# Outer taps of an MLP's depthwise convolution: over two sequences at once, with the two tokens at their border computed apart

## The chip, the cores and the metric

The kernel runs on one core of a Trainium2 chip. Its engines are TensorE (PE; PEld is its weight load), VectorE (DVE), ScalarE (ACT), GpSimd (POOL) and SyncE (SP), which issues all DMAs here. Each engine works through its own queue in order and waits on semaphores for the others. The metric is the device time of one execution in microseconds; the time of a kernel is the median of its runs.

## What is computed

Two layers of an encoder trunk run over two sequences with shared weights, one of 512 tokens and one of 256. Each layer has a mixer (state-space scan, retention, neighbourhood attention, gates) and then a gated MLP; only the MLP matters here. The convolution has three taps along the tokens of one sequence, each feature by itself, and zeros beyond both ends, so that nothing crosses from one sequence to the other.

```python
def dwconv(x, w, bias):                       # width 3, centred, per channel, zero padding
    ...
h2 = rmsnorm(x, norm_ffn)
u = dwconv(h2 @ ffn_w_up, ffn_conv_w, ffn_conv_b)       # 1024 -> 2 x 2816
val, gt = jnp.split(u, 2, axis=-1)
x = x + (jax.nn.silu(gt) * val) @ ffn_w_down            # 2816 -> 1024
```

## The kernel before

Both sequences lie side by side as T = 768 columns: columns 0 to 511 are the first (TP = 512), 512 to 767 the second. In the MLP the features stand on the 128 partitions and the tokens on the free axis. The 2816 features of each half are 22 tiles of 128, and `up(i)` makes one tile of the value half (`rv`) and one of the gate half (`rg`) together; one such call is called a unit below.

- **Products.** `pair_products` (L500) computes both tiles by a Strassen-like scheme: seven products of 12 matmuls each (`prod`, L489 to L494), 384 columns wide, which accumulate in PSUM tiles `acc` named X, Y, V, Z. The weights are split in two float32r parts, `whi` by ACT (L206) and `wlo` by DVE (L207), after DVE has formed sums of weight blocks in place (L217, L229). ACT and DVE take the results out of PSUM and combine them (all recorded at L498): into `pt`, `rv` and `rg`.
- **Convolution.** `conv(1)` treats `rg`, later `conv(0)` treats `rv`. ACT writes the middle tap and the bias for all 768 columns (L1285). DVE adds the left tap (L1287) and then the right one (L1289), each for the two sequences apart: 511 and 255 columns, since the first token of a sequence has no left neighbour and the last no right one. That makes four DVE operations for each tile. The gate half goes through Silu on ACT (L1293). Behind the value half DVE multiplies both (L1296), ACT rounds the product to `ah` (L1297) and DVE makes the remainder `al` (L1298).
- **Down projection.** Units are taken in groups of three (the last group of a layer has four): when a group's `ah` and `al` are there, PE multiplies them with the down weights into PSUM tiles `dn` (L1342 to L1344, 512 columns wide) and DVE adds these to `x` (L1357). The first unit of the next group is computed ahead of a group's down projection. In the last group of a layer eight `dn` tiles are begun with the first three units, and the last unit is added when it is there.

The order on each engine is not the order of the source: when the program is built, a scheduler with its own time model picks, from what the program's order and its priorities allow, the instruction to place next. So another set of instructions gives another interleaving. There are 2 x 22 = 44 units, hence 88 convolutions and 352 operations at L1287 and L1289.

Of the kernel before, what the change touches and what calls it, by code (L numbers as in the profile page):

```python
# [9 lines left out]
AF = mybir.ActivationFunctionType  # L10
OP = mybir.AluOpType

P = 128
# [3 lines left out]
TP = 512  # L17
TS = 256
T = TP + TS
# [264 lines left out]
def body(tc, nc, a, depth=DEPTH):  # L284
# [8 lines left out]
    act, tt, stt, ts = (nc.scalar.activation, nc.vector.tensor_tensor,  # L293
                        nc.vector.scalar_tensor_tensor, nc.vector.tensor_scalar)
# [79 lines left out]
    RANGES = ((0, TP), (TP, TS))  # L374
# [34 lines left out]
    def st4(name):  # L409
        return base.tile([P, 1024], F32, name=name, tag="st4", bufs=2)  # L410

    def small(shape, name, bufs=4):
        return base.tile(shape, F32, name=name, tag="sm_" + name, bufs=bufs)
# [174 lines left out]
    def layer(l, x_in, prev_x):  # L588
# [633 lines left out]
        for b in range(3):  # L1222
            dst, k0 = oT[b]
            r = [h[:, k0:k0 + 4, :] for h in dst]
# [28 lines left out]
        def ftile(name, tag, bufs=1, dt=F32):  # L1253
            return (ap if tag in ("ah", "al") else fp).tile([P, T], dt, name=name, tag=tag, bufs=bufs)
# [20 lines left out]
        def up(i):  # L1275

            raw = [ftile("rv", "rv"), ftile("rg", "rg")]
            us = {}
            out = [ftile("ah", "ah", 4, F32R), ftile("al", "al", 4, F32R)]

            def conv(s):
                r, u = raw[s], ftile("u", ("uv", "ug")[s])
                f = i + NFF * s
                w = lambda j: par[:, O_FW + f * 3 + j:O_FW + f * 3 + j + 1]
                act(u, r, AF.Identity, scale=w(1), bias=par[:, O_FB + f:O_FB + f + 1])  # L1285
                for c0, n in RANGES:
                    stt(u[:, c0 + 1:c0 + n], r[:, c0:c0 + n - 1], w(0), u[:, c0 + 1:c0 + n],  # L1287
                        op0=OP.mult, op1=OP.add)
                    stt(u[:, c0:c0 + n - 1], r[:, c0 + 1:c0 + n], w(2), u[:, c0:c0 + n - 1],  # L1289
                        op0=OP.mult, op1=OP.add)  # L1290
                us[s] = u
                if s == 1:
                    act(u, u, AF.Silu)  # L1293
                    return
                ah, al = out
                tt(u, u, us[1], op=OP.mult)  # L1296
                act(ah, u, AF.Copy)  # L1297
                tt(al, u, ah.bitcast(F32), op=OP.subtract)  # L1298

            pair_products(*raw, st4("pt"), conv, "po", first=todo[0]() if i == 0 else None)  # L1300
            return out
# [23 lines left out]
        for gi, g in enumerate(DOWN_GROUPS):  # L1325
# [9 lines left out]
            ws, n, end = W.get(len(g)), len(g), gi == len(DOWN_GROUPS) - 1  # L1335
# [64 lines left out]
```

## Time and profile before

| | |
|---|---|
| three runs | 2604.86, 2606.41, 2600.97 us; median 2604.86 us |
| the profiled execution | 2605.65 us, of which the traced span is 2603.9 us |
| PE busy in the span | 2560.1 us (98%) |
| DVE busy | 1904.2 us (73%) |
| ACT busy | 1153.4 us (44%) |
| POOL busy | 87.8 us (3%) |
| granted TensorE clock, mean | 0.995 of full speed |

The span is the traced part of one execution; the profiled execution's own time is 1.75 us longer than it. Busy times of one engine overlap with those of the others, so their shares don't add up. Matmuls are recorded longer than the distance at which they follow each other, since they are pipelined: whether PE has a pause is read from the starts.

### The profile page before, as it was taken

The page shows a single profiled execution, that of the slowest core. Times are in us where ns is not written, and L with a number is a line of the kernel's source. Part 1 is how long each engine was busy: PE and PEld are TensorE (multiplying, and loading weights), DVE is VectorE, ACT ScalarE, POOL GpSimd, SP SyncE. Part 2 cuts the span into 40 slices and gives each one's busy share as a digit, 9 for nine tenths or more (in the row PEclk, how much of TensorE's full clock was granted, in tenths as well). Part 3 has the DMA queues.
Part 4 walks back from the last instruction along what each step waited for, and adds up shares of the span by engine and source line. Part 5 has one row for each costly group of instructions (what it writes and reads, how often), then busy time and mean ns, then how long its engine had stood idle before and what let it go on. Part 6 is the DMA issues. An engine that isn't in the chain of part 4 may idle for free.

```text
span 2603.9 us, 37538 instructions
## 1 busy us (share of the span) xinstructions
PE 2560.1 (98%) x14290; PEld 2353.6 (90%) x14290; DVE 1904.2 (73%) x3204; ACT 1153.4 (44%) x1946; POOL 87.8 (3%) x130
## 2 busy tenths in 40 slices
PE   8999999999999999999999999999999999999998
PEld 8878999999889999999998789999998899999997
DVE  6758876665658887888866688765657598888887
ACT  5434465553235433333454455655432354333343
POOL 0002100000000000000000011100000000000000
PEclk9999999999999999999999999999999999999999
DMA  7356568747522222222453575787474222212222
GB/s 248 108 169 204 190 213 255 223 134 230 158 81 67 67 70 73 65 68 71 135 174 129 163 233 172 219 236 215 132 230 141 73 89 65 62 60 73 74 66 89
DMA packets 168900, 359.65 MB, mean 138 GB/s; under 512 B 16080, under 2 KB 62480, under 8 KB 168720
## 3 DMA queue, kind: packets, MB, share of 16 engines
q1 hardware_dynamic: 168720, 357.25, 43.5%
q8 instruction: 113, 1.85, 0.3%
q14 instruction: 67, 0.55, 0.1%
HBM read 276.87 MB, written 80.31 MB: 137 GB/s over the span
## 4 chain that ended last, share of the span: by engine, by line
PE 85%; DMA 7%; ACT 3%; DVE 3%; issue 1%; SPq 1%; POOL 0%; DVEq 0%; POOLq 0%; ACTq 0%
PE acc L493 12%; PE acc L492 12%; PE acc L494 12%; PE dn L1344 5%; PE dn L1342 5%; PE dn L1343 5%; PE acc L366 4%; PE acc L368 4%; PE acc L367 4%; PE acc L389 3%; PE acc L388 3%; PE acc L390 3%; PE wo L390 2%; PE wo L388 2%; PE wo L389 2%
## 5 line engine op out<-in xcount | busy, mean ns | idle before, releaser
L206 ACT ACTIVATE whi<-wraw 128x1024 fp32r<-128x1024 f32 (+2 forms) x444 | 433.8, 985 | 616.0 <-DMA wraw<-wp 153.3
L207 DVE TENSOR_TENSOR wlo<-wraw,whi 128x1024 fp32r<-128x1024 f32 (+2 forms) x444 | 500.3, 1132 | 189.2 <-ACT whi L206 186.9
L493 PE MATMUL acc<-hTl,whi 128*128 128x384 f32 x1216 | 414.3, 341 | 5.0 <-DVE hTl L435 5.0
L492 PE MATMUL acc<-hTh,whi 128*128 128x384 f32 x1216 | 414.1, 341 | 2.9 <-ACT pt L498 2.0
L494 PE MATMUL acc<-hTh,wlo 128*128 128x384 f32 x1216 | 410.0, 339 | 0.0
L492 PE MATMUL acc<-Eh,whi 128*128 128x384 f32 x912 | 309.3, 340 | 0.9 <-DVE pv L498 0.9
L494 PE MATMUL acc<-Eh,wlo 128*128 128x384 f32 x912 | 307.4, 338 | 0.0
L493 PE MATMUL acc<-El,whi 128*128 128x384 f32 x912 | 306.9, 337 | 0.0
L493 PEld LDWEIGHTS acc<-hTl,whi 128*128 128x128 f32 x1216 | 230.3, 189 | 7.5 <-DVE hTl L435 6.0
L492 PEld LDWEIGHTS acc<-hTh,whi 128*128 128x128 f32 x1216 | 229.9, 189 | 7.4 <-ACT pt L498 3.5
L494 PEld LDWEIGHTS acc<-hTh,wlo 128*128 128x128 f32 x1216 | 229.9, 189 | 0.4
L389 PE MATMUL acc<-wlo,hTh 128*128 128x512 f32 (+1 forms) x576 | 210.1, 366 | 2.6 <-DVE wlo L207 2.6
L388 PE MATMUL acc<-whi,hTh 128*128 128x512 f32 (+1 forms) x576 | 208.8, 364 | 2.9 <-ACT whi L206 2.6
L390 PE MATMUL acc<-whi,hTl 128*128 128x512 f32 (+1 forms) x576 | 209.2, 365 | 0.0
L1343 PE MATMUL dn<-wlo,ah 128*128 128x512 f32 x528 | 207.4, 393 | 0.0
L1344 PE MATMUL dn<-whi,al 128*128 128x512 f32 x528 | 201.8, 394 | 0.0
L1342 PE MATMUL dn<-whi,ah 128*128 128x512 f32 x528 | 200.4, 393 | 0.0
L1357 DVE TENSOR_TENSOR x<-x,dn 128x512 f32<-128x512 f32 x168 | 111.9, 685 | 86.0 <-PE dn L1344 86.0
L366 PE MATMUL acc<-hTh,whi 128*128 128x256 f32 (+1 forms) x512 | 174.0, 340 | 0.0
L492 PEld LDWEIGHTS acc<-Eh,whi 128*128 128x128 f32 x912 | 171.3, 188 | 2.9 <-DVE pv L498 1.9
L368 PE MATMUL acc<-hTh,wlo 128*128 128x256 f32 (+1 forms) x512 | 172.9, 338 | 0.0
L367 PE MATMUL acc<-hTl,whi 128*128 128x256 f32 (+1 forms) x512 | 172.9, 338 | 0.0
(277 smaller groups left out, 4772.3 us busy)
## 6 DMA issues: line engine op xcount, KB each, us to landing
wraw<-wp SPq DMA_DIRECT2D x284, 512.0 KB
g<-gate_scr SPq DMA_DIRECT2D x48, 384.0 KB
cw<-cum_scr SPq DMA_DIRECT2D x48, 256.0 KB
xt<-xbc_scr SPq DMA_DIRECT2D x20, 512.0 KB
bias<-nab SPq DMA_DIRECT2D x40, 256.0 KB
gate_scr<-pg SPq DMA_DIRECT2D x24, 384.0 KB
gate_scr<-pv SPq DMA_DIRECT2D x24, 384.0 KB
ot<-o_scr SPq DMA_DIRECT2D x36, 256.0 KB
```

The lines of the kernel that those rows point to most:

```text
L206: self.nc.scalar.activation(hi[:, :n], r, AF.Copy)
L207: self.nc.vector.tensor_tensor(lo[:, :n], r, hi[:, :n].bitcast(F32), op=OP.subtract)
L366: mm(o, wh[:, k, :], rh, start=(k == 0), stop=False)
L388: mm(o, hT[0][:, k, ts_], wh[:, cs], start=(k == 0), stop=False)
L389: mm(o, hT[0][:, k, ts_], wl[:, cs], start=False, stop=False)
L390: mm(o, hT[1][:, k, ts_], wh[:, cs], start=False, stop=(k == NK - 1))
L492: mm(o, w[0][:, k, :], r[0][:, k, :], start=first and k == 0, stop=False, skip_group_check=True)
L493: mm(o, w[0][:, k, :], r[1][:, k, :], start=False, stop=False, skip_group_check=True)
L494: mm(o, w[1][:, k, :], r[0][:, k, :], start=False, stop=k == 3, skip_group_check=True)
L1342: mm(ps, ah[:, tsl], wh[:, cs], start=(j == 0), stop=False)
L1343: mm(ps, ah[:, tsl], wl[:, cs], start=False, stop=False)
L1344: mm(ps, al[:, tsl], wh[:, cs], start=False, stop=(j == n - 1))
```

## The change

In `conv`, each outer tap becomes one DVE operation over 767 columns that runs through the border between the sequences (L1290 and L1291 of the new program). At the border this would add to column 512 (first token of the second sequence) a left neighbour that isn't its own, and to column 511 (last token of the first) a right one. So ACT computes these two columns apart: column 511 with its left tap alone into `end[:, 0]` (L1288) and column 512 with its right tap alone into `end[:, 1]` (L1289), from the middle tap's result before DVE has changed it. Behind both taps ACT copies `end` over the two columns of `u` (L1292). Lines below the change are two higher: Silu is L1295, the multiply L1298, `ah` L1299, `al` L1300.

```diff
                 act(u, r, AF.Identity, scale=w(1), bias=par[:, O_FB + f:O_FB + f + 1])
-                for c0, n in RANGES:
-                    stt(u[:, c0 + 1:c0 + n], r[:, c0:c0 + n - 1], w(0), u[:, c0 + 1:c0 + n],
-                        op0=OP.mult, op1=OP.add)
-                    stt(u[:, c0:c0 + n - 1], r[:, c0 + 1:c0 + n], w(2), u[:, c0:c0 + n - 1],
-                        op0=OP.mult, op1=OP.add)
+
+                end = small([P, 2], "nmx", 3)
+                act(end[:, 0:1], r[:, TP - 2:TP - 1], AF.Identity, scale=w(0), bias=u[:, TP - 1:TP])
+                act(end[:, 1:2], r[:, TP + 1:TP + 2], AF.Identity, scale=w(2), bias=u[:, TP:TP + 1])
+                stt(u[:, 1:], r[:, :T - 1], w(0), u[:, 1:], op0=OP.mult, op1=OP.add)
+                stt(u[:, :T - 1], r[:, 1:], w(2), u[:, :T - 1], op0=OP.mult, op1=OP.add)
+                act(u[:, TP - 1:TP + 1], end, AF.Copy)
                 us[s] = u
```

For each of the 88 convolutions two DVE operations go and three ACT operations come. The scheduler also interleaves the MLP's instructions on PE, DVE and ACT anew. Outside the two MLPs the order on all engines stays what it was, and on SP and POOL the order stays the same throughout, the MLPs included.

The end of DVE's queue in the last unit of layer 1, before (names in brackets are the engines or DMA queues whose semaphores a row waits for):

```order
L1287 SCALAR_TENSOR_TENSOR u<-rg,par,u 128x511 [waits Activation_49]
L1287 SCALAR_TENSOR_TENSOR u<-rg,par,u 128x255
L1289 SCALAR_TENSOR_TENSOR u<-rg,par,u 128x511 [waits DVE_49]
L1289 SCALAR_TENSOR_TENSOR u<-rg,par,u 128x255 [waits DVE_49]
L498 SCALAR_TENSOR_TENSOR rv<-acc,pt 128x384 [waits PE_49]
L1287 SCALAR_TENSOR_TENSOR u<-rv,par,u 128x511 [waits Activation_49]
L1287 SCALAR_TENSOR_TENSOR u<-rv,par,u 128x255
L1289 SCALAR_TENSOR_TENSOR u<-rv,par,u 128x511 [waits DVE_49]
L1289 SCALAR_TENSOR_TENSOR u<-rv,par,u 128x255 [waits DVE_49]
L1296 TENSOR_TENSOR u<-u 128x768 [waits DVE_49]
L1298 TENSOR_TENSOR al<-u,ah 128x768 [waits Activation_49]
```

The same place of DVE's queue after the change:

```order
L1290 SCALAR_TENSOR_TENSOR u<-rg,par,u 128x767 [waits Activation_49]
L1291 SCALAR_TENSOR_TENSOR u<-rg,par,u 128x767 [waits DVE_49]
L498 SCALAR_TENSOR_TENSOR rv<-acc,pt 128x384 [waits PE_49]
L1290 SCALAR_TENSOR_TENSOR u<-rv,par,u 128x767 [waits Activation_49]
L1291 SCALAR_TENSOR_TENSOR u<-rv,par,u 128x767 [waits DVE_49]
L1298 TENSOR_TENSOR u<-u 128x768 [waits DVE_49,Activation_49]
L1300 TENSOR_TENSOR al<-u,ah 128x768 [waits Activation_49]
```

The four taps of each half became two, and the multiply now waits for ACT too.

ACT's queue in the third unit of layer 0, before (`rg` and `rv` are the unit's gate and value tiles, `whi` the weight splits of units to come):

```order
L1285 ACTIVATE u<-rg,par 128x768
L206 ACTIVATE whi<-wraw 128x1024 [waits DMAHW0_49]
L1285 ACTIVATE u<-rv,par 128x768 [waits DVE_49,Activation_49]
L206 ACTIVATE whi<-wraw 128x1024 [waits DMAHW1_49,PE_49]
L1293 ACTIVATE u<-u 128x768 [waits DVE_49,Activation_49]
L206 ACTIVATE whi<-wraw 128x1024 [waits DMAHW2_49,PE_49]
L498 ACTIVATE rv<-acc 128x384 [waits DVE_49,PE_49,Activation_49]
```

The same unit on ACT after the change:

```order
L1285 ACTIVATE u<-rg,par 128x768
L1288 ACTIVATE nmx<-rg,u,par 128x1 [waits Activation_49]
L1289 ACTIVATE nmx<-rg,u,par 128x1
L206 ACTIVATE whi<-wraw 128x1024 [waits DVE_49,PE_49]
L206 ACTIVATE whi<-wraw 128x512 [waits DMAHW4_49,PE_49]
L1292 ACTIVATE u<-nmx 128x2 [waits DVE_49,Activation_49]
L1295 ACTIVATE u<-u 128x768 [waits Activation_49]
L1285 ACTIVATE u<-rv,par 128x768 [waits DVE_49]
```

The two small operations follow the middle tap, and the copy waits for DVE's second tap with Silu directly behind it. Over the whole program the row behind L1292 is Silu or its table load 41 times, `ah` 27 times, `whi` 12 times, a PSUM tile's evacuation (L498) 6 times and a middle tap twice.

## Rows read from the trace of the kernel before

**Rows 1.** The head of the profile page: span, busy time of each engine, and the granted TensorE clock in 40 slices (tenths of full speed).

```profile
span 2603.9 us, 37538 instructions
PE 2560.1 (98%) x14290; PEld 2353.6 (90%) x14290; DVE 1904.2 (73%) x3204; ACT 1153.4 (44%) x1946; POOL 87.8 (3%) x130
...
PEclk9999999999999999999999999999999999999999
```

**Rows 2.** Busy time by stretch, in the MLP of layer 0 and in that of layer 1: stretch, its length, then busy us and number of instructions for PE, PEld, DVE, ACT and POOL, the granted clock, the share of the DMA engines and GB/s.

```profile
805.00:1280.00 475.00, 475.00 (x2493) 444.79 (x2492) 393.32 (x587) 198.03 (x237) 0.00 (x0) 1.00 0.24 73
2105.00:2565.00 460.00, 460.00 (x2415) 431.17 (x2414) 381.58 (x570) 188.40 (x226) 0.00 (x0) 1.00 0.23 71
```

**Rows 3.** Groups of PE's instructions by line and shape in the stretch 805 to 1280 us: count, then busy us, mean ns of one, and idle time of PE before them. The three groups of the down projection's matmuls; all others are the 384 wide ones of the products.

```profile
L1343 PE MATMUL dn<-wlo,ah 128*128 128x512 f32 x232 | 91.2, 393 | 0.0
L1344 PE MATMUL dn<-whi,al 128*128 128x512 f32 x232 | 89.4, 394 | 0.0
...
L1342 PE MATMUL dn<-whi,ah 128*128 128x512 f32 x232 | 87.6, 393 | 0.0
```

**Rows 4.** PE's timeline (start us, duration us, instruction): the first and the last of 24 matmuls of 384 columns in a row, and the first and the last of the 48 matmuls of 512 columns that end the program's PE work.

```profile
816.84 0.34 PE L492 MATMUL acc<-hTh,whi 128*128 128x384 f32 x1
...
820.89 0.34 PE L494 MATMUL acc<-hTh,wlo 128*128 128x384 f32 x1
...
2585.16 0.40 PE L1342 MATMUL dn<-whi,ah 128*128 128x512 f32 x1
...
2596.03 0.40 PE L1344 MATMUL dn<-whi,al 128*128 128x512 f32 x1
```

**Rows 5.** Groups of DVE's instructions by shape over the whole span, the outer taps alone: count, busy us, mean ns, idle time before them and what ended it.

```profile
L1287 DVE SCALAR_TENSOR_TENSOR u<-rv,par,u 128x511 f32<-128x511 f32 x44 | 32.9, 748 | 8.1 <-ACT u L1285 8.1
...
L1289 DVE SCALAR_TENSOR_TENSOR u<-rv,par,u 128x255 f32<-128x255 f32 x44 | 21.1, 480 | 0.0
```

**Rows 6.** Groups of ACT's instructions by shape over the whole span, with the same columns: weight splits of two widths, the middle tap, and the narrowest operation there is.

```profile
L206 ACT ACTIVATE whi<-wraw 128x1024 fp32r<-128x1024 f32 x360 | 381.7, 1060 | 598.2 <-DMA wraw<-wp 153.3 <-PE dn L1344 102.7 <-PE acc L367 80.1
...
L206 ACT ACTIVATE whi<-wraw 128x512 fp32r<-128x512 f32 x76 | 47.2, 621 | 16.3 <-PE acc L493 14.7 <-PE acc L390 1.6
...
L1285 ACT ACTIVATE u<-rv,par 128x768 f32<-128x768 f32 x44 | 45.2, 1028 | 20.1 <-DVE rv L498 19.9
...
L957 ACT ACTIVATE tk<-tk 128x8 f32<-128x8 f32 x2 | 0.4, 198 | 0.0
```

**Rows 7.** ACT's timeline: a pair of weight splits (1024 and 512 columns, merged into one row) at 820 us, and the value half of the last unit of layer 1. In brackets the idle time before a row and what ended it.

```profile
820.02 1.56 ACT L206 ACTIVATE whi<-wraw 128x1024 fp32r<-128x1024 f32 x2
...
2572.82 1.03 ACT L1285 ACTIVATE u<-rv,par 128x768 f32<-128x768 f32 x1 [1.36 <-DVE rv L498]
2577.12 0.85 ACT L1297 ACTIVATE ah<-u 128x768 fp32r<-128x768 f32 x1 [3.27 <-DVE u L1296]
```

**Rows 8.** DVE's timeline at the same place: both parts of a tap are merged into one row.

```profile
2573.89 1.15 DVE L1287 SCALAR_TENSOR_TENSOR u<-rv,par,u 128x511 f32<-128x511 f32 x2 [1.10 <-ACT u L1285]
2574.95 1.14 DVE L1289 SCALAR_TENSOR_TENSOR u<-rv,par,u 128x511 f32<-128x511 f32 x2
2576.12 0.96 DVE L1296 TENSOR_TENSOR u<-u 128x768 f32<-128x768 f32 x1
2578.00 0.96 DVE L1298 TENSOR_TENSOR al<-u,ah 128x768 fp32r<-128x768 f32 x1 [0.91 <-ACT ah L1297]
```

**Rows 9.** PE's timeline at the same place: the last matmul of the units before the last one, the first with the last unit's `ah`, and the eight with its `al`.

```profile
2579.41 0.40 PE L1344 MATMUL dn<-whi,al 128*128 128x512 f32 x1
2579.64 0.40 PE L1342 MATMUL dn<-whi,ah 128*128 128x512 f32 x1
...
2583.32 1.99 PE L1344 MATMUL dn<-whi,al 128*128 128x512 f32 x8
```

**Rows 10.** ACT's timeline at two places of layer 0: a pair of weight splits (1024 and then 512 columns) in the middle of the MLP, and `ah` of the last unit.

```profile
1114.32 1.56 ACT L206 ACTIVATE whi<-wraw 128x1024 fp32r<-128x1024 f32 x2
...
1284.12 0.85 ACT L1297 ACTIVATE ah<-u 128x768 fp32r<-128x768 f32 x1 [3.52 <-DVE u L1296]
```

**Rows 11.** PE's timeline at these two places: the first matmul that reads the wider `whi` of that pair, and, at the end of layer 0, the last matmul of the earlier units and the first that reads the last unit's `ah`.

```profile
1115.99 0.34 PE L492 MATMUL acc<-Eh,whi 128*128 128x384 f32 x1
...
1285.52 0.39 PE L1344 MATMUL dn<-whi,al 128*128 128x512 f32 x1
1285.75 0.39 PE L1342 MATMUL dn<-whi,ah 128*128 128x512 f32 x1
```

**Rows 12.** Waits between engines in the stretch 805 to 1295 us, ACT's waits for DVE's convolution work: waiting engine, what it was about to do, for whom, total us, times, longest us.

```profile
ACT ah L1297 <- DVE u L1296: 38.4, 14, 5.6
...
ACT u L1293 <- DVE u L1289: 14.7, 8, 3.3
...
ACT rv L498 <- DVE u L1289: 10.9, 9, 3.5
```

**Rows 13.** PE's own waits in the stretch 760 to 1330 us, which holds the MLP of layer 0 with its beginning and its end: the same columns.

```profile
PE acc L493 <- DVE hTl L435: 2.5, 2, 1.8
PE acc L388 <- DVE zst L630: 0.3, 1, 0.3
PE acc L492 <- ACT hTh L434: 0.2, 1, 0.2
```

## The prediction

> **What bounds the kernel now.** I read the busy shares first: PE is busy for 2560.1 of 2603.9 us at full clock, DVE for 1904.2 and ACT for 1153.4 [rows 1]. That is an average over stages, so next come the two stretches in which the convolutions run, one for each layer. There PE is busy for all of 475 and all of 460 us, at a granted clock of 1.00, which is the upper of its two levels, 2.4 GHz [rows 2]. DVE is next with 393 of 475 us (83%), ACT has 198 (42%) [rows 2].
>
> A busy PE need not be PE at its peak, since matmuls are recorded longer than the distance at which they follow each other. So I count them. The first stretch holds 2493 matmuls [rows 2], of which 3 x 232 = 696 are 512 wide [rows 3] and 1797 are 384 wide. Where nothing disturbs, 24 narrow ones start from 816.84 to 820.89 us: 4.05 / 23 = 0.176 us apart. 48 wide ones start from 2585.16 to 2596.03: 10.87 / 47 = 0.231 apart [rows 4]. 1797 x 0.176 + 696 x 0.231 = 316 + 161 = 477 us, in a stretch of 475. It holds as many matmuls as fit; there is no hidden pause to win. Around it PE waits 3.0 us in all, for the normalization that precedes the first unit, and for the next layer's input projection, never for a convolution [rows 13]. So PE's matmul count sets the time of both MLPs, and the change leaves this count alone.
>
> **The change, part by part.** *DVE, removed.* A tap of 511 columns takes 0.748 us and one of 255 takes 0.480 [rows 5], so 256 columns cost 0.268 us and one of 767 will take 0.748 + 0.268 = 1.016. The busy sum falls by 0.748 + 0.480 - 1.016 = 0.212 us for each of 176 merged taps, 37 us in all. What the queue gains is less, because operations that follow each other overlap: the two of L1287 take 1.15 us together [rows 8], not 1.228, so both taps go from 2573.89 to 2574.95 + 1.14 = 2576.09, 2.20 us, and become 2 x 1.016 - 0.08 = 1.95. DVE wins 0.25 us a convolution, 22 us over 88. All of it lies beside PE's work; on the path it is worth nothing.
>
> *ACT, added.* No ACT row shows a single column with a scale and a bias per partition; two rows bound it. The narrowest operation takes 0.198 us [rows 6], but without them. The weight splits cost (1.060 - 0.621) / 512 = 0.000857 us a column, so the middle tap's 1.028 for 768 columns has a fixed part of 0.370 [rows 6]. L1288 and L1289 have the middle tap's form, so I take 0.37 each, and 0.20 for the plain copy of two columns: 0.94 us a convolution, 83 us over 88. Two that follow each other overlap by 1.060 + 0.621 - 1.56 = 0.12 us [rows 6, 7]. ACT goes from 42% of an MLP's stretch to about 51%; it stays far from full.
>
> *The path of one convolution.* For the value half of the last unit of layer 1, ACT begins the middle tap at 2572.82, DVE the multiply at 2576.12, and ACT `ah` at 2577.12 [rows 7, 8]. New on this path: L1288 waits for the middle tap on its own engine, so it comes whole (0.37), and L1289 overlaps (0.25), since DVE's left tap now waits for it. The taps take 0.25 less. Then L1292 (0.20) with one crossing from DVE to ACT and one back; a crossing takes 0.04 us, from 2573.85 to 2573.89 [rows 7, 8]. Sum: 0.62 - 0.25 + 0.28 = +0.65 us. Bounds: +0.2 if the small operations take 0.2 and overlap fully, +1.2 if every crossing costs 0.2 more. A gain is excluded, since a crossing to ACT and back is added and only 0.25 goes.
>
> *Who waits for that path.* PE does, at the start of the last unit's matmuls. In layer 1 `ah` is there at 2577.97 [rows 7] and PE asks for it at 2579.64 [rows 9]: 1.67 us spare. `al` is there at 2578.96 [rows 8], and PE asks at 2583.32 [rows 9]. In layer 0 `ah` ends at 1284.97 [rows 10] and PE asks at 1285.75: 0.78 us spare [rows 11]. Both margins hold +0.65. At +1.2 the second would be passed by 0.4 us. The other groups have the whole first unit of the next group as cover, 84 x 0.176 = 14.8 us.
>
> *Who stands behind the new wait.* L1292 holds ACT's queue until DVE's second tap is done. In 68 of 88 places Silu, its table load or `ah` stands next, which waited for the convolution before as well; in 12 places it is a weight split, in 6 an evacuation of PSUM. ACT has waited up to 3.3 us for the same tap ahead of Silu, up to 3.5 ahead of an evacuation and up to 5.6 for the multiply [rows 12], and PE did not pause for any of that. The tightest weight split that I found has less room: it ends at 1114.32 + 1.06 = 1115.38 [rows 6, 10] and PE reads it at 1115.99 [rows 11], 0.61 us later. If all 0.94 us of added ACT work stood ahead of such a split, PE would lose 0.33 us there. I take none, because the scheduler lays the order out again and DVE's queue is freer, and 14 x 0.33 = 4.6 us (once for each group of units) as the upper bound.
>
> *Sum.* PE's work: 0. Ends of layers: 0 (at most 0.4). Weight splits: 0 (at most 4.6). On the profiled execution's own 2605.65 us this gives 2605.65 to 2610.7. That execution lies 0.8 us over the median of 2604.86, which moves the forecast to 2604.9, rounded to **2605**.
>
> **The rivals.** *Slower: the border tokens put ACT on PE's path.* Mechanism: the convolution's path becomes 0.65 us longer in each unit, and ACT, held in L1292, brings a split or an evacuation late to PE. Price: 44 x 0.65 = 29 us if every unit pays it, 2634; if one unit in each of the 14 groups does, 9 us, 2614. It decides from the point at which PE pauses for 5.2 / 44 = 0.12 us a unit. For it speaks the margin of 0.61 us; against it that waits of 3 to 5 us on ACT cost PE nothing.
>
> *Faster: PE has room that DVE's relief opens.* If the pace of the MLP were set by DVE, at 83% the next engine, its 22 us would come back: 2605 - 22 = 2583. Against it stands the count above: 477 us of matmuls in 475. In these stretches weight loads are busy for 444.79 of 475 us, 94% [rows 2]. The Trainium skill ("Perfetto Trace Analysis", section "Identifying the Most-Contended Engine") judges PE's headroom by that share and not by matmul busy time; by its rule 6% of the stretch, some 30 us, would still be open, and the faster case would stand. The trace disagrees: a 512 wide matmul holds PE for 0.231 us whatever its weight load takes, so the share is under one without a pause.
>
> *The taps don't get cheaper.* If 767 columns took the full 1.228 us, DVE would win nothing. That alone leaves the time at 2605, and belongs to the forecast.
>
> **How the numbers follow.** A difference under 0.2% (5.2 us) can't be told from no change in this kernel, whose three runs spread over 5.4 us. Forecast, no change: 0.88, from 2601 (the spread of runs) to 2610. Slower rival: 0.08, 2611 to 2634. Faster rival: 0.02, near 2583. The last 0.02 is a measurement that lands off by over 0.2% for no cause of the change, half on each side. So faster 0.03, same 0.88, slower 0.09. The range of 8 in 10 takes in the spread below and the bound of the splits above: 2600.5 to 2609.5.
>
> **What would show it.** Right: PE busy for the whole of both stretches again, with 2493 matmuls in some 475 us; L1290 and L1291 near 1.02 us, 88 of each; L1288 and L1289 near 0.37, L1292 near 0.20; DVE's busy sum down by some 37 us and ACT's up by some 83; spare time ahead of the last `ah` shorter by about 0.65 us. Wrong: waits of PE for `whi`, `ah` or an evacuated PSUM tile inside the stretches, above all right behind an L1292 on ACT, or stretches that shrink.

## The result and the profile after

The changed kernel takes 2619.54 us (median of 4 runs, 2615.71 to 2622.59) beside 2603.09 for the kernel before on the same chip (4 runs, 2600.97 to 2606.41). The ratio is 1.0058, interval [1.0038, 1.0078]: slower by 0.58%, some 16 us, where no change was forecast. The profiled execution took 2621.53 us with a span of 2619.7, against 2605.65 and 2603.9 before: +15.8 us of span.

The head of the page after [rows 1]:

```profile
span 2619.7 us, 37637 instructions
...
PE 2567.1 (98%) x14290; PEld 2357.2 (90%) x14290; DVE 1888.1 (72%) x3028; ACT 1218.8 (47%) x2210; POOL 88.9 (3%) x130
...
PEclk9999999999999999999999999999999999999999
```

It tells nearly nothing of the loss: PE has as many matmuls, DVE is less busy by 16 us, ACT more by 65, and the clock's 40 slices look untouched. The new operations cost what was forecast. These are their groups over the whole span (count: shortest/median/longest ns, first and last start), where [rows 5] and [rows 6] gave the forecast:

```profile
L1292 ACT ACTIVATE u<-nmx x88: 185/198/213, 830.0 to 2592.9; 128x2 f32<-128x2 f32 x88
...
L1288 ACT ACTIVATE nmx<-rg,u,par x44: 369/379/390, 824.1 to 2585.1; 128x1 f32<-128x1 f32 x44
L1289 ACT ACTIVATE nmx<-rg,u,par x44: 371/375/382, 824.4 to 2585.4; 128x1 f32<-128x1 f32 x44
...
L1290 DVE SCALAR_TENSOR_TENSOR u<-rg,par,u x44: 1007/1012/1020, 825.2 to 2585.8; 128x767 f32<-128x767 f32 x44
...
L1291 DVE SCALAR_TENSOR_TENSOR u<-rg,par,u x44: 1008/1018/1021, 827.0 to 2586.8; 128x767 f32<-128x767 f32 x44
```

The busy time by stretch shows where to look (columns as in [rows 2]):

```profile
805.00:1280.00 475.00, 470.25 (x2456) 440.54 (x2456) 379.45 (x496) 224.40 (x357) 0.00 (x0) 0.99 0.23 69
2105.00:2565.00 460.00, 455.84 (x2380) 426.52 (x2379) 368.33 (x480) 215.42 (x345) 0.00 (x0) 1.00 0.22 67
...
800.00:850.00 50.00, 44.57 (x236) 43.48 (x235) 41.39 (x57) 26.55 (x42) 0.00 (x0) 0.93 0.23 71
850.00:1280.00 430.00, 430.00 (x2245) 401.03 (x2244) 341.43 (x444) 199.62 (x319) 0.00 (x0) 1.00 0.23 70
2100.00:2150.00 50.00, 45.33 (x248) 44.41 (x247) 41.87 (x59) 27.42 (x45) 0.00 (x0) 0.97 0.25 79
2150.00:2565.00 415.00, 415.00 (x2158) 386.27 (x2157) 330.49 (x429) 190.34 (x305) 0.00 (x0) 1.00 0.22 67
```

PE, full in both stretches before, now lacks 4.75 and 4.16 us, all of it ahead of 850 and 2150 us. Behind that it is busy for 430 of 430 and 415 of 415 us. So the loss is not spread over 44 units; it happens once in each layer, at the start. PE's waits name it with a row that the kernel before does not have:

```profile
PE acc L492 <- DVE rg L498: 8.4, 2, 4.2
```

Two waits of 4.2 us. PE's timeline at the one of layer 0: the last matmul ahead of it, and the first three behind.

```profile
826.16 0.34 PE L494 MATMUL acc<-Eh,wlo 128*128 128x384 f32 x1
830.71 0.66 PE L492 MATMUL acc<-hTh,whi 128*128 128x384 f32 x1 [4.21 <-DVE rg L498]
831.17 0.52 PE L493 MATMUL acc<-hTl,whi 128*128 128x384 f32 x1
831.49 0.52 PE L494 MATMUL acc<-hTh,wlo 128*128 128x384 f32 x1
```

Behind the pause matmuls start 0.32 us apart, not 0.176 [rows 4]. The granted clock tells why (stretches of 2 us, the clock is the third number from the right):

```profile
830.00:832.00 2.00, 1.29 (x4) 1.32 (x5) 2.00 (x4) 1.97 (x4) 0.00 (x0) 0.50 0.79 254
832.00:834.00 2.00, 2.00 (x8) 2.00 (x7) 1.35 (x3) 0.98 (x4) 0.00 (x0) 0.50 0.02 8
834.00:836.00 2.00, 2.00 (x8) 2.00 (x8) 2.00 (x4) 1.77 (x3) 0.00 (x0) 0.50 0.02 4
836.00:838.00 2.00, 2.00 (x12) 2.00 (x11) 1.97 (x4) 0.83 (x3) 0.00 (x0) 0.89 0.00 0
838.00:840.00 2.00, 2.00 (x13) 2.00 (x12) 1.41 (x2) 0.93 (x2) 0.00 (x0) 1.00 0.00 0
```

After the pause PE runs at 1.2 GHz, the lower level, from 830.71 to about 836.4 us. That is 5.7 us at half pace, 2.9 us lost; with the pause of 4.21 and one of 0.53 at 819.87, 7.6 us in layer 0. In layer 1 the pause is 4.16 us and the half clock lasts for only some 3.4 us behind it (granted 0.53 and 0.62 in the two stretches from 2130 to 2134 us), 1.7 us lost and 5.9 in all. The busy column hides the half clock: 2.00 of 2.00 us with 8 matmuls, where the stretch from 838 to 840 us at full clock has 13 (a matmul that reaches over an edge counts on both sides).

What DVE did meanwhile shows on its own timeline. Here are taps of the first unit and the evacuation of the second unit's first gate product (`rg<-acc,pt`), with which PE's pause ends. First the kernel before, whose MLP starts 2.1 us earlier in its span (the output projection's last matmul starts at 788.68 us before and at 790.81 after):

```profile
812.35 1.14 DVE L1287 SCALAR_TENSOR_TENSOR u<-rv,par,u 128x511 f32<-128x511 f32 x2
813.40 1.14 DVE L1289 SCALAR_TENSOR_TENSOR u<-rv,par,u 128x511 f32<-128x511 f32 x2
...
826.62 0.55 DVE L498 TENSOR_TENSOR rg<-acc,pt 128x384 f32<-128x384 f32 x1
```

And the changed kernel:

```profile
817.33 1.23 DVE L207 TENSOR_TENSOR wlo<-wraw,whi 128x1024 fp32r<-128x1024 f32 x1 [2.30 <-ACT whi L206]
...
825.16 1.01 DVE L1290 SCALAR_TENSOR_TENSOR u<-rg,par,u 128x767 f32<-128x767 f32 x1
826.09 1.01 DVE L1290 SCALAR_TENSOR_TENSOR u<-rv,par,u 128x767 f32<-128x767 f32 x1
827.02 1.01 DVE L1291 SCALAR_TENSOR_TENSOR u<-rg,par,u 128x767 f32<-128x767 f32 x1
827.95 1.22 DVE L207 TENSOR_TENSOR wlo<-wraw,whi 128x1024 fp32r<-128x1024 f32 x1
829.08 1.01 DVE L1291 SCALAR_TENSOR_TENSOR u<-rv,par,u 128x767 f32<-128x767 f32 x1
830.01 0.55 DVE L498 TENSOR_TENSOR rg<-acc,pt 128x384 f32<-128x384 f32 x1
```

Before, the values' taps (`rv`) run at 812, in a gap. After, DVE idles in that gap (2.30 us ahead of 817.33), and all four taps, with a weight split among them, stand right ahead of the evacuation.

The evacuation itself is hardly late, however. Counted from the output projection's last matmul it starts at 37.9 us before and at 39.2 us after, 1.3 us later, beside a pause of 4.2. What moved far is the second unit's other evacuation, that of its values on ACT, from 26.0 to 41.4 us by the same count. Before and after:

```profile
814.66 0.50 ACT L498 ACTIVATE rv<-acc 128x384 f32<-128x384 f32 x1
```

```profile
832.21 0.48 ACT L498 ACTIVATE rv<-acc 128x384 f32<-128x384 f32 x1
```

In the code `rv` has one buffer. So this evacuation has to wait until the first unit's taps have read `rv`, a wait that [rows 12] shows too; until it is done, one of the three PSUM banks for `acc` stays full. Before, it came right behind the last of the value taps (813.40 + 1.14). After, PE does one product of 12 matmuls less ahead of the pause: from 816.84 us before there are 24 in a row that read `hTh` or `hTl` [rows 4], and here 12, up to the row of 822.10.

```profile
819.87 0.45 PE L492 MATMUL acc<-hTh,whi 128*128 128x384 f32 x1 [0.53 <-DVE pt L498]
...
822.10 0.41 PE L492 MATMUL acc<-Eh,whi 128*128 128x384 f32 x1
```

So PE runs out of banks earlier and then stands until `rg<-acc,pt` gives one back. This link, from the late taps to the pause, is read from the traces and the code; no run gave `rv` a second buffer. All kernels timed below agree with it: PE has 12 such matmuls there in both MLPs of the three whose values wait for the ring, and 24 in all others.

ACT's timeline shows what held the values' taps back:

```profile
813.77 1.03 ACT L1285 ACTIVATE u<-rv,par 128x768 f32<-128x768 f32 x1
...
821.60 1.59 ACT L206 ACTIVATE whi<-wraw 128x1024 fp32r<-128x1024 f32 x2 [4.30 <-DVE wraw L217]
...
824.13 0.39 ACT L1288 ACTIVATE nmx<-rg,u,par 128x1 f32<-128x1 f32 x1
824.43 0.37 ACT L1289 ACTIVATE nmx<-rg,u,par 128x1 f32<-128x1 f32 x1
824.71 0.37 ACT L1288 ACTIVATE nmx<-rv,u,par 128x1 f32<-128x1 f32 x1
```

The values' middle tap starts at 813.77, but their border product L1288 only at 824.71, straight behind those of the gates, although ACT idles for 4.30 us in between. No data make it wait. What the two halves share is the tile `end`: every one comes from one ring of three buffers (the tag "nmx"), and the code writes the gates' convolution ahead of the values', though in the first unit of an MLP the values are ready first.

**Ring theory.** The scheduler hands a ring's tiles out in the order in which the code first writes them. The values' `end` stands second, so in the first unit it can't be had until the gates' half is ready some 10 us later. This makes the values' taps late, and with them the evacuation into `rv`. **Work theory** (the slower rival of the prediction): the border products, the longer path of a convolution or the coarser 1.01-us taps cost time themselves. **Re-weaving**: any added operations make the scheduler order the start in another way.

### The profile page after: what moved, and what is told of

It is laid out like the page before. It is cut to its first block, busy times and chain, and to the rows that moved or that the text cites. A ratio compares the mean times of both kernels' runs of the same rounds, so it can differ in the third digit from the quotient of the medians.

```text
span 2619.7 us, 37637 instructions
## 1 busy us (share of the span) xinstructions
PE 2567.1 (98%) x14290; PEld 2357.2 (90%) x14290; DVE 1888.1 (72%) x3028; ACT 1218.8 (47%) x2210; POOL 88.9 (3%) x130
## 4 chain that ended last, share of the span: by engine, by line
PE 84%; DMA 7%; DVE 4%; ACT 3%; issue 2%; SPq 0%; POOL 0%; DVEq 0%; ACTq 0%; POOLq 0%
PE acc L492 12%; PE acc L493 12%; PE acc L494 12%; PE dn L1346 5%; PE dn L1344 5%; PE dn L1345 5%; PE acc L366 4%; PE acc L368 4%; PE acc L367 4%; PE acc L389 4%; PE acc L390 4%; PE acc L388 4%; DMA wraw<-wp 2%; PE npo L1124 2%; PE wo L390 1%
```

## The experiments

Each is timed beside the kernel before on the same chip. "MLP" is the time from the start of the output projection's last matmul to the start of the down projection's last one, read from PE's timeline, for layer 0 and layer 1.

| kernel | median us | ratio to before | MLP us |
|---|---|---|---|
| before | | | 514.6, 513.8 |
| after | 2619.5 | 1.0058 [1.0038, 1.0078] | 523.3, 520.9 |
| two rings | 2606.5 | 1.0005 [0.9993, 1.0018] | 516.3, 515.4 |
| old taps in the first units | 2605.7 | 1.0005 [0.9995, 1.0015] | 515.2, 514.8 |
| new taps in the first units alone | 2619.9 | 1.0060 [1.0044, 1.0077] | 523.3, 521.8 |
| old taps, tile from one ring | 2617.4 | 1.0052 [1.0037, 1.0067] | 522.0, 519.5 |
| old taps, tile from two rings | 2607.0 | 1.0010 [1.0001, 1.0019] | 517.0, 514.6 |
| one ring, values written first | 2607.8 | 1.0011 [1.0002, 1.0019] | 516.8, 515.9 |
| two rings, border work twice | 2615.2 | 1.0035 [1.0021, 1.0050] | 521.5, 520.5 |
| two rings, border work three times | 2636.4 | 1.0120 [1.0103, 1.0137] | 529.7, 530.3 |
| merge alone | 2608.1 | 1.0013 [1.0003, 1.0022] | 516.6, 516.6 |

The MLPs grew by 8.7 and 7.1 us, together the 15.8 us of span; what the other stages gained and lost cancels. The code cuts below are against the changed kernel, and differences of indentation are left out.

**Two rings.** The values' `end` gets a ring of its own ("ssq2" is the tag of a small tile that exists already):

```diff
-                end = small([P, 2], "nmx", 3)
+                end = small([P, 2], ("ssq2", "nmx")[s], (4, 3)[s])
```

> Same work as the changed kernel; only `end` comes from two rings (one for the values' half, one for the gates' half) in place of one. Ring theory: in the first unit the values' border operations and merged taps run as early as in the kernel before (near 813 us in layer 0, 2112 us in layer 1), TensorE has no pause of over 1 us and no stretch at half clock at the start of either MLP, and the time is that of the kernel before or a little under it, 2599 to 2605 us. Work theory (the longer conv on ScalarE, or the 1.01-us taps as coarser pieces on VectorE, cost in themselves): the time stays at 2614 to 2623 us.

1.0005: the loss is gone, with every border product and merged tap in place. ACT's and then DVE's timeline show the values' half early again:

```profile
809.43 1.03 ACT L1285 ACTIVATE u<-rv,par 128x768 f32<-128x768 f32 x1
810.50 0.39 ACT L1288 ACTIVATE ssq<-rv,u,par 128x1 f32<-128x1 f32 x1
```

```profile
811.19 1.02 DVE L1290 SCALAR_TENSOR_TENSOR u<-rv,par,u 128x767 f32<-128x767 f32 x1 [0.51 <-ACT ssq L1289]
```

PE is busy for 49.92 and 49.73 us of the first 50 at full clock (44.57 and 45.33 with one ring):

```profile
800.00:850.00 50.00, 49.92 (x285) 49.42 (x284) 43.40 (x59) 29.63 (x46) 0.00 (x0) 1.00 0.24 74
...
2100.00:2150.00 50.00, 49.73 (x277) 48.37 (x276) 44.46 (x58) 30.39 (x49) 0.00 (x0) 1.00 0.32 95
```

The work theory is out as the cause of the 16 us.

**Old taps in the first units, and new taps in the first units alone.** `conv` takes the new or the old body by the unit's number `i`; in the second kernel the condition is `i == 0`:

```diff
+                if i > 0:
                     end = small([P, 2], "nmx", 3)
...
                     act(u[:, TP - 1:TP + 1], end, AF.Copy)
+                else:
+                    for c0, n in RANGES:
+                        stt(u[:, c0 + 1:c0 + n], r[:, c0:c0 + n - 1], w(0), u[:, c0 + 1:c0 + n],
...
```

> The old four taps in the first unit of each MLP, the new taps in the other 42 of the kernel's 44 units. Ring theory (the loss sits in the first unit alone): 2599 to 2605 us, no pause at the start. Work theory, with a cost in every unit: 42 of 44 of the loss stays, 2614 to 2623 us.

> The new taps in the first unit of each MLP alone, the old four taps in the other 42 units. Ring theory: nearly all of the loss is here, 2615 to 2623 us, with the pause of 4 us and the half clock after it at both starts. Work theory, with a cost in every unit: 2 of 44 of the loss, 2602 to 2606 us.

1.0005 and 1.0060. The 42 other units cost nothing that can be measured, and the two first ones the whole loss, again with waits of 4.18 and 4.15 us at the starts.

**Old taps, tile from one ring.** The tile without its use: nothing reads `end`, and the taps are those of the kernel before.

```diff
                 end = small([P, 2], "nmx", 3)
-                act(end[:, 0:1], r[:, TP - 2:TP - 1], AF.Identity, scale=w(0), bias=u[:, TP - 1:TP])
...
-                act(u[:, TP - 1:TP + 1], end, AF.Copy)
+                act(end, u[:, TP - 1:TP + 1], AF.Copy)
+                for c0, n in RANGES:
+                    stt(u[:, c0 + 1:c0 + n], r[:, c0:c0 + n - 1], w(0), u[:, c0 + 1:c0 + n],
...
```

> The old four taps in every unit; added is only one small ScalarE copy per half of the two tokens at the joint into an `end` tile from the one shared ring (0.2 us each, 88 in all; nothing reads `end`). Ring theory: the ring by itself holds the values' taps of the first unit back until the gates' half is ready, so a pause of TensorE appears at the start of both MLPs though the taps are the old ones: 2608 to 2621 us. Work theory: nothing of the merged taps and of the border products is here, 2601 to 2606 us.

1.0052: 88 copies of 0.2 us into tiles that nobody reads cost nearly what the whole change cost. PE's timeline has the pauses again:

```profile
828.79 0.41 PE L492 MATMUL acc<-hTh,whi 128*128 128x384 f32 x1 [3.07 <-DVE rg L498]
...
2126.58 0.66 PE L492 MATMUL acc<-hTh,whi 128*128 128x384 f32 x1 [3.00 <-DVE rg L498]
```

On DVE one of the values' four taps runs early and three are late:

```profile
813.73 0.48 DVE L1289 SCALAR_TENSOR_TENSOR u<-rv,par,u 128x255 f32<-128x255 f32 x1
...
827.43 0.74 DVE L1291 SCALAR_TENSOR_TENSOR u<-rv,par,u 128x511 f32<-128x511 f32 x1
828.10 0.55 DVE L498 TENSOR_TENSOR rg<-acc,pt 128x384 f32<-128x384 f32 x1
...
2125.88 0.55 DVE L498 TENSOR_TENSOR rg<-acc,pt 128x384 f32<-128x384 f32 x1
```

This run also shows that the pause does not need a late `rg<-acc,pt`. From the output projection's last matmul (789.70 and 2088.52 us) it starts at 38.4 us in layer 0 and at 37.4 us in layer 1, beside 37.9 and 37.6 us in the kernel before, whose row in layer 1 is this one (from 2082.27):

```profile
2119.82 0.55 DVE L498 TENSOR_TENSOR rg<-acc,pt 128x384 f32<-128x384 f32 x1
```

Yet PE pauses for 3.07 and 3.00 us. The evacuation `rv<-acc` on ACT starts at 40.0 and 38.9 us here, and at 26.0 and 25.6 in the kernel before.

**The same with two rings.** It parts the ring from the mere addition of operations; the edit is the line of the first experiment.

> The old four taps and the small ScalarE copy of the run before with one shared ring, in every unit, but with a ring for each half. Ring theory: the values' taps of the first unit run early again, no pause of over 1 us at the start of the MLPs, 2601 to 2607 us. If it is the 88 added ScalarE copies, or just any re-weaving of the schedule by added instructions, that cost 13 us there: 2612 to 2621 us.

1.0010 against 1.0052 for the same 88 copies: re-weaving by added operations does not do it, the shared ring does.

**One ring, values written first.** The front of `conv` (middle tap, tile, border products) becomes a function `head`; in the first unit the code writes the values' ahead of the gates':

```diff
+            heads = {}
+            def head(s):
...
+                heads[s] = r, u, w, end
+
             def conv(s):
+                for h in (0, 1) if i == 0 else (s,):
+                    if h not in heads:
+                        head(h)
+                r, u, w, end = heads[s]
```

> The changed kernel with its one ring and the same instructions; only the middle tap and the border products of the first unit's values are written in the code ahead of those of its gates. Ring theory, told closer (the one ring is handed out in the order in which its tiles are first written in the code, and the values' tile stood second): values' taps early, no pause, 2601 to 2607 us. If a second ring matters in itself (more slots, one more free buffer), or the merged taps do: 2614 to 2623 us, as in the changed kernel.

1.0011, and no wait of PE on `rg`; `rv<-acc` starts at 28.2 and 28.6 us from the output projection's last matmul, beside 41.4 and 40.6 in the changed kernel. The instructions are those of the changed kernel, and so is the ring. Only the order of writing differs. A second ring is not needed, and more buffers are not what was lacking.

**Border work three times and twice.** Two rings, and L1288 and L1289 repeated, with `range(2)` in the second kernel:

```diff
+                for _ in range(3):
                     act(end[:, 0:1], r[:, TP - 2:TP - 1], AF.Identity, scale=w(0), bias=u[:, TP - 1:TP])
                     act(end[:, 1:2], r[:, TP + 1:TP + 2], AF.Identity, scale=w(2), bias=u[:, TP:TP + 1])
```

> The changed kernel with two rings, and each of the two border products done three times (four more ScalarE operations of 0.37 us per conv, 1.5 us on its path, 130 us of ScalarE time in all). Ring theory, in which the border work itself costs nothing while TensorE's queue has cover: 2601 to 2609 us. Work theory: the path of a conv is lengthened by more than twice what the change added (0.65 us); if that was near its margin, TensorE stands in each unit or at each group's end, and the time goes over 2620 us.

> The changed kernel with two rings, and each of the two border products done twice (two more ScalarE operations of 0.37 us per conv, 0.75 us on its path, 65 us of ScalarE time in all). It asks how far the cover of the border work reaches, after three times cost 32 us. If the cover ends between one and two times: over 2612 us, with TensorE's pause of the first unit back or short waits in later units. If it ends between two and three times: 2601 to 2609 us.

1.0120 and 1.0035: the first went over 2620 us, as the work theory had it for this run and not the ring theory. The cover of the border work ends between one and two times its size. With it twice, PE loses 3 and 2 us in the first 50 us, and about 2 us of each rest of an MLP, in short waits that the two-ring kernel hardly has. These are some of its waits:

```profile
PE acc L492 <- ACT rv L498: 3.7, 4, 1.0
...
PE acc L492 <- DVE pt L498: 2.6, 2, 1.5
...
PE acc L492 <- ACT ssq L1290: 1.1, 2, 0.6
```

L1290 is the second border product in that program, so the last row names the border work itself as what PE waited for. So the mechanism of the slower rival exists; at the size of the change it does not yet take hold. With three times the pause of 4 us at the first unit is back as well, though the rings are two; by its timeline `rv<-acc` is early there (30.7 us from the output projection's last matmul) and the gates' taps and `rg<-acc,pt` are late (43.8 us), behind ACT's longer queue, but no run tested that. Whether the added path or ACT's added busy time counts was not parted.

**Merge alone.** Without the border products, the tile and the copy back, so that the two tokens at the joint get a neighbour's product that is not theirs:

```diff
-                end = small([P, 2], "nmx", 3)
-                act(end[:, 0:1], r[:, TP - 2:TP - 1], AF.Identity, scale=w(0), bias=u[:, TP - 1:TP])
-                act(end[:, 1:2], r[:, TP + 1:TP + 2], AF.Identity, scale=w(2), bias=u[:, TP:TP + 1])
                 stt(u[:, 1:], r[:, :T - 1], w(0), u[:, 1:], op0=OP.mult, op1=OP.add)
                 stt(u[:, :T - 1], r[:, 1:], w(2), u[:, :T - 1], op0=OP.mult, op1=OP.add)
-                act(u[:, TP - 1:TP + 1], end, AF.Copy)
```

> Left out: the border products, their tile and the copy back; the merged taps run straight over the joint, so the two tokens there get a neighbour's product that is not theirs. What is left of the change is the cheaper taps alone: 22 us less VectorE time, no ScalarE time added, no ring. If relief of VectorE beside a full TensorE is worth nothing: 2601 to 2607 us. If the cheaper taps do bring time that the border work then took back: under 2598 us. If it is the one-piece taps that block VectorE's queue: 2612 to 2621 us with the pause at the start.

1.0013: the cheaper taps bring nothing, not even with no work added. DVE's busy time is 1885.2 us here, 19 less than before, and the time is no shorter.

## Why the prediction was wrong

**The step that failed is "who waits".** It measured spare time at the ends of the layers and at the weight splits, and gave all other groups "the whole first unit of the next group as cover". The start of each MLP was never looked at. There no earlier unit's matmuls cover the first convolution, and its taps stand between PE and its next PSUM banks, since `rv` and `rg` can be filled anew only behind them. [Rows 13] showed only that PE had no wait there before, not by how much. The second half of the failure is the sentence on the weight splits, "because the scheduler lays the order out again and DVE's queue is freer": the new layout was taken as harmless, when it was what cost the time here. The tile `end` was costed by its operations and not as a place in a shared ring. And the price of a pause was left at its length: with the slow clock behind them the pauses make 7.6 and 5.9 us of the 8.7 and 7.1 that the MLPs grew by. The rest, 1.1 and 1.2 us, is in the range by which the kernels without the pause are longer too.

**The prices were right.** 1.016 us a merged tap was forecast, 1.01 came; 0.37 and 0.20 for the border operations came as 0.375 to 0.379 and 0.198. By their durations the taps lost 176 x (0.748 + 0.480 - 1.015) = 37.5 us, 37 forecast. DVE's queue was to win 22 us; its busy time, in which an overlap counts once, fell by 16.1. ACT's added operations sum to 88 x (0.379 + 0.375 + 0.198) = 84 us, 83 forecast; the page shows 65.4 more, since it counts overlapping operations once. The path of the last convolution of layer 1, from the start of the middle tap to that of `ah`, grew from 4.30 us [rows 7] to 2594.09 - 2588.94 = 5.15, +0.85 where +0.65 was forecast with bounds of +0.2 and +1.2.

**PE's count sets the MLP** held where the scheduler's order let it: PE was full behind the first 50 us of both, and the merge alone gave nothing. The faster rival is thus refuted by a run: with 19 us less on DVE the time did not fall. The room that the Trainium skill ("Perfetto Trace Analysis", section "Identifying the Most-Contended Engine") would read from weight loads busy for 94% of the stretch was not there to take.

**The slower rival** named times (2614 to 2634) that hold the result, but by another mechanism. That they hold it is luck: the changed kernel's border work on its own lost nothing that could be told in the run with two rings. The rival's point of decision, however, was nearer than argued: twice the border work is past it.

**What stays open.** Three of the repaired or reduced kernels lie 0.10 to 0.13% over the kernel before, two 0.05%, and their MLPs are 0.6 to 2.8 us longer. It appears with old taps and with new ones, with a ring and without, so no single part of the change explains it. The intervals of the three just exclude 1, those of the two do not; what it comes from stays open. That the scheduler ties the values to the gates through the ring is inferred from three runs that break the tie in two ways; its inner rules were not looked at. No version beat the kernel before.

## What to carry to other kernels

A new temporary is not only its instructions: taken from a shared ring, it ties operations that had nothing to do with each other into the order in which the code writes them, and the engine then idles with ready work behind it. Where two halves become ready in another order than they are written, give each its own ring, or write the one that is ready first ahead.

Where the bottleneck engine is full, check the margins at the start of each stage as well as at the end: the first unit has no earlier work as cover, and one late evacuation there costs a pause and the slow clock behind it. The instruction that ends a wait need not be the one that caused it: ask of every bank or buffer that was full at that moment what kept it full.

## What was unexpected of the hardware

A pause of 4.21 us at 826.5 to 830.7 us was followed by a granted clock of 0.50 for 5.7 us, in a stage whose clock is otherwise 1.00, and one of 4.16 us in layer 1 by half clock for only some 3.4 us; pauses of 3.07 and 3.00 us (old taps, tile from one ring) were followed by mean clocks of 0.67 and 0.57 in the four microseconds that hold their ends. With the border work twice, a pause of 1.50 us that ended at 819.89 left the clock at 1.00:

```profile
816.00:820.00 4.00, 2.50 (x15) 2.17 (x13) 3.38 (x5) 1.14 (x3) 0.00 (x0) 1.00 0.25 102
820.00:824.00 4.00, 4.00 (x23) 4.00 (x24) 3.37 (x6) 1.65 (x4) 0.00 (x0) 1.00 0.02 4
```
